# A decoder step in f32: fixed TensorE order in the prompt attention, gated products kept in PSUM, two tiles normed by VectorE

## The chip, the cores and the metric

One core of a Trainium2 chip runs one program. The metric is the time of one execution in device microseconds (us). The engines are PE (TensorE), DVE (VectorE), ACT (ScalarE), POOL (GpSimd) and SP (which issues most DMAs); PSUM has eight banks of 128 partitions, each of which takes 512 f32 columns here.

## The reference

One layer of a hybrid decoder serves a prompt of 1024 tokens and eight sample requests of eight tokens over paged caches. Cut to what matters here:

```
h  = x * (1 + scale1) + shift1
P  = h @ w_in                                  # conv part, queries, keys, values, gates
o  = gates * (compressed, selected and sliding-window attention)
x  = LN1(ALPHA * x + gate1 * (concat(rms(conv), rms(o)) @ w_o))
h2 = x * (1 + scale2) + shift2
x  = LN2(ALPHA * x + gate2 * (silu(h2 @ w_gate) * (h2 @ w_up)) @ w_down)
LN(x) = (x - mean(x)) * rsqrt(var(x) + EPS) * g + b
```

D_MODEL is 1024, the hidden width of the SwiGLU is 2816 (22 blocks of 128), there are 12 query heads of 64 over 2 key/value groups, and the sliding window is 512 keys. Everything is f32.

## The kernel before, in words

The stages follow one another: sample attention and compression to about 840 us, projections to 1041, the prompt attention (`phase_prompt`) to about 1441, `w_o` and the first norm to about 1565, and the feed-forward part with the second norm (`phase_ffn`) to the end.

**Prompt attention.** The work is cut into 32 units, a block i of 128 queries with one key/value group and one half of its heads; units go in 16 pairs. For each pair, `window()` interleaves two lists: the scores of the next pair and the values of this one. A chunk of scores is two matmuls into a bank of the pool `psS` (`khh`, then `kll`, lhsT are keys, `qs` the queries) and a DVE reduction (L1224) that adds the mask, takes the maximum and writes S to SBUF. ACT makes the exponentials (L1235), POOL combines the weights (L1247). `values()` then has, for each 128 keys, `tr(n)`: three PE transposes of S into a bank of `psPT` (L95) and one copy to an SBUF buffer `PT` of the pool `tp` (L1299, by ACT or DVE in turn); and `mm(n)`: two matmuls of PT with the values V, one into each half of the partitions of the one bank `psPO` (f32 rows, `V`, or `Vpc` for the compressed ones). `evac` and `out` take psPO out and turn it. The eight PSUM banks are psS 4, psPT 3, psPO 1. `both()` gives each value step a place LA steps behind its transposes, and a weight. These numbers (LA, FRONT, LEAD) set the order in which the code emits the work; a list scheduler then orders each engine's instructions by its own costs.

**Feed-forward.** The hidden blocks go in GROUPS: eight of two blocks and two of three. `down(n, i)` does one group for one tile i of 128 tokens: for each half of the 512 columns 6 (or 9) matmuls into one of five banks (psFD and psFG in turn), a DVE product with the gate (L1902) from PSUM to the SBUF row buffer `spare`, and a DVE `scalar_tensor_tensor` (L1903) that adds it into x. The last group goes by the order `g2 u2 g0 NT 6 u0 7 g1 0 1 u1 2 3 4 5`: gate and up blocks, and tiles by number (NT is the tile of the samples). After each tile's down, `finish(i)` takes the statistics (L1913, L1914) and `center()` (ACT square root, two small DVE operations L1650 and L1651, ACT identity L1652) makes x - mean times rstd in place; `write(i)`, one tile later, applies gain and bias (`affine`: POOL on the first columns at L1659 and DVE on the rest at L1661, 896 and 128 of 1024, but 768/256 for tile 4 and 256/768 for tile 5) and sends the tile out (L1921).

In the rows, `qo` names the rows of a tile of x (and `spare`), `fr` the gain and bias of the norm, `fst` the statistics, `fw`/`F` weights and hidden values, `gate1p` the gate.

Of the kernel before, what the change touches and what calls it, by code (L numbers as in the profile page):

```python
# [48 lines left out]
class _Step:  # L49
# [1121 lines left out]
    def phase_prompt(self):  # L1171
        nc, tc = self.nc, self.tc
        with ExitStack() as cx:
            pool = lambda n, b, **k: cx.enter_context(self.pool(n, b, **k))
            qp, tp = pool("pq", 6), pool("pt", 5)
            sp = [None, pool("pS1", 3)]
# [4 lines left out]
            extra = op.tile([P, D], F32, name="extra", tag="extra", bufs=1)  # L1181
            psS, psT, psO = (pool(n, b, space=PSUM) for n, b in (("psS", 4), ("psPT", 3), ("psPO", 1)))
            st = {}
# [154 lines left out]
            def both(a, b):  # L1338

                LA = 3  # L1340
                ta, ma, ea, oa = values(a)
                tb, mb, eb, ob = values(b)
                steps, at = [], {}
                for base, m in ((0, ma), (len(ta), mb)):
                    for k, f in enumerate(m):
                        at.setdefault(base + 2 * k + LA, []).append((0.7, f))
                end = 2 * len(ma) - 2 + LA
                at.setdefault(end, []).append((0.0, ea))
                at.setdefault(end + 3, []).append((0.4, oa))
                t = ta + tb  # L1350
                n = 0
                while n < len(t) or any(k >= n for k in at):
                    if n < len(t):
                        steps.append((0.33, t[n]))
                    steps += at.get(n, [])
                    n += 1
                return steps, [eb, ob]

            def window(sc, va, tail):

                tot = sum(x[0] or 0 for x in sc) + sum(x[0] for x in va)
                ev = [(0.1 + 1.4 * n, f) for n, f in enumerate(tail)]
                if sc:
# [18 lines left out]

            FRONT, LEAD = 0.6, 2.0
            for n in range(2):
# [5 lines left out]
            for n, pair in enumerate(pairs):  # L1390
# [4 lines left out]
                v, t = both(*pair)  # L1395
                window(nxt, v, tail)
                tail = t
# [248 lines left out]
    def center(self, x, m, st):  # L1646
# [3 lines left out]
        nc.vector.reciprocal(st[0:m, 15:16], st[0:m, 14:15])  # L1650
        nc.vector.scalar_tensor_tensor(st[0:m, 14:15], st[0:m, 12:13], -1.0, st[0:m, 15:16], op0=ALU.mult, op1=ALU.mult)  # L1651
        nc.scalar.activation(x[0:m, :], x[0:m, :], AF.Identity, bias=st[0:m, 14:15], scale=st[0:m, 15:16])  # L1652
# [146 lines left out]
    def phase_ffn(self):  # L1799
        nc, tc, I, O = self.nc, self.tc, self.I, self.O  # L1800
        gl = self.gl2
        with ExitStack() as cx:
# [84 lines left out]
            def down(n, i):  # L1887
# [3 lines left out]
                for h in range(2):  # L1891
                    c = slice(512 * h, 512 * h + 512)
                    ps = any_bank()
                    for j in range(a, b):
# [4 lines left out]
                        else:  # L1899
                            self.mm2(ps[:], f[:, T:TA + BS], w[:, 0, c], w[:, 1, c], j == a, j == b - 1)  # L1900
                    t = spare[:, c]
                    nc.vector.tensor_tensor(t, ps[:], g[:, c], op=ALU.mult)  # L1902
                    nc.vector.scalar_tensor_tensor(x[:, c], x[:, c], ALPHA if n == 0 else 1.0, t,  # L1903
                                                   op0=ALU.mult, op1=ALU.add)

            def finish(i):
# [7 lines left out]
                nc.vector.bn_aggr(st[0:m, 12:14], st[0:m, 0:12].rearrange("p (n c) -> p n c", n=2))  # L1914
                self.center(x, m, st)

            def write(i):
                m, x = P if i < NT else BS, self.x1[i]
                self.affine(x, m, *ln2, {5: (256, 256), 4: (768, 768)}.get(i, (896, 896)))
                dst = O[0][0, P * i:P * i + P, :] if i < NT else O[1].rearrange("b t d -> (b t) d")  # L1920
                nc.sync.dma_start(dst, x[0:m, :])  # L1921
# [48 lines left out]
            def last(i):  # L1970
                down(len(self.GROUPS) - 1, i)
                finish(i)
                if before:
                    write(before.pop())
                before.append(i)

            steps = ("g2", "u2", "g0", NT, 6, "u0", 7, "g1", 0, 1, "u1", 2, 3, 4, 5)
            for x in steps:
# [3 lines left out]
                else:  # L1982
                    last(x)
            write(before.pop())

# [70 lines left out]
```

## Time and profile before

| what | us |
|---|---|
| time, median of 3 runs | 2389.46 (2388.64 to 2394.4) |
| the profiled execution's own time | 2393.08 |
| its span | 2391.3 |
| PE busy | 2293.0, 96% of the span |
| DVE / ACT / POOL busy | 1429.6 / 920.1 / 851.7 |
| granted PE clock, mean | 0.99 |

Shares of busy time are averages over stages. The chain of work that ended last, followed back from the last instruction, lies on PE for 84% of the span and on DVE for 6%. In the 40 slices of the page PE is at nine tenths or more nearly everywhere; the last slice has four tenths. A start and a length of each instruction are printed by the timeline; PE's matmuls overlap, so the time that one takes from the path is the distance from its start to the start of the next, not its length.

### The profile page before, as it was taken

The page shows a single profiled execution, that of the slowest core. Times are in us where ns is not written, and L with a number is a line of the kernel's source. Part 1 is how long each engine was busy: PE and PEld are TensorE (multiplying, and loading weights), DVE is VectorE, ACT ScalarE, POOL GpSimd, SP SyncE. Part 2 cuts the span into 40 slices and gives each one's busy share as a digit, 9 for nine tenths or more (in the row PEclk, how much of TensorE's full clock was granted, in tenths as well). Part 3 has the DMA queues.
Part 4 walks back from the last instruction along what each step waited for, and adds up shares of the span by engine and source line. Part 5 has one row for each costly group of instructions (what it writes and reads, how often), then busy time and mean ns, then how long its engine had stood idle before and what let it go on. Part 6 is the DMA issues. An engine that isn't in the chain of part 4 may idle for free.

```text
span 2391.3 us, 38693 instructions
## 1 busy us (share of the span) xinstructions
PE 2293.0 (96%) x14834; PEld 1901.9 (80%) x14834; DVE 1429.6 (60%) x3407; ACT 920.1 (38%) x2108; POOL 851.7 (36%) x912
## 2 busy tenths in 40 slices
PE   5999999989999999999999999999999999999994
PEld 3777778778888788976566657889999999999893
DVE  4654766667777530167888776656554456552558
ACT  0232343348888512267767765331111111111122
POOL 6676766621111221244444453422212222212224
PEclk9999999999999999999999999999999999999997
DMA  9778555547665233100000013021111111111111
GB/s 285 263 269 281 201 169 175 172 160 267 249 249 220 84 132 82 47 28 1 1 1 1 1 45 102 28 61 45 45 36 53 45 45 45 45 36 54 41 37 68
DMA packets 139119, 249.23 MB, mean 104 GB/s; under 512 B 13507, under 2 KB 109741, under 8 KB 134774
## 3 DMA queue, kind: packets, MB, share of 16 engines
q0 software_dynamic: 23312, 138.36, 16.1%
q1 hardware_dynamic: 113446, 107.35, 14.5%
q8 instruction: 117, 1.92, 0.3%
q10 hardware_dynamic: 2176, 1.05, 0.2%
q14 instruction: 68, 0.56, 0.1%
HBM read 239.23 MB, written 11.63 MB: 105 GB/s over the span
## 4 chain that ended last, share of the span: by engine, by line
PE 84%; DVE 6%; DMA 2%; issue 2%; ACT 2%; POOL 2%; another core or an unknown queue 1%; SPq 0%; POOLq 0%; DVEq 0%; ACTq 0%
PE psFG L75 15%; PE psA L75 12%; PE psFU L75 11%; PE psM L75 7%; PE psPA L75 7%; PE psPO L75 6%; PE psS L75 5%; PE psFD L75 5%; PE psPT L95 5%; PE psST L95 4%; PE psWA L75 3%; PE psSO L75 2%; DVE qo L1661 1%; PE psM L95 1%
## 5 line engine op out<-in xcount | busy, mean ns | idle before, releaser
L72 POOL TENSOR_TENSOR fw<-fr,fw 128x1024 fp32r<-128x1024 f32 x64 | 160.9, 2520 | 584.8 <-ACT fw L66 584.8
L75 PE MATMUL psFU<-h,fw 128*128 128x384 f32 (+1 forms) x1056 | 252.5, 324 | 0.0
L75 PE MATMUL psFG<-h,fw 128*128 128x384 f32 (+1 forms) x1008 | 241.0, 324 | 0.0
L1247 POOL TENSOR_SCALAR S<-S,stat 128x64 f32<-128x64 f32 (+8 forms) x288 | 168.6, 602 | 191.4 <-DVE stat L1244 101.6
L623 DVE STREAM_TRANSPOSE XT<-X 128x1024 f32<-128x1024 f32 x128 | 158.9, 1242 | 124.5 <-PE psA L75 105.0
L66 ACT CAST fw<-fr 128x1024 fp32r<-128x1024 f32 x65 | 67.6, 1054 | 412.7 <-issue 305.4
L75 PEld LDWEIGHTS psFU<-h,fw 128*128 128x128 f32 x1056 | 190.6, 187 | 0.7
L625 POOL TENSOR_TENSOR XS<-XT 128x512 f32<-128x512 f32 x120 | 154.3, 1287 | 100.5 <-DVE XT L623 82.9
L1873 DVE TENSOR_TENSOR sl<-sl,psFU 128x384 f32<-128x384 f32 (+1 forms) x66 | 31.5, 527 | 259.9 <-PE psFU L75 257.6
L75 PEld LDWEIGHTS psFG<-h,fw 128*128 128x128 f32 x1008 | 182.2, 187 | 0.3 <-ACT sl L1861 0.2
L1235 ACT ACTIVATE S<-S,stat 128x64 f32<-128x64 f32 (+8 forms) x288 | 171.5, 598 | 18.7 <-DVE stat L1233 16.7
L1903 DVE SCALAR_TENSOR_TENSOR qo<-qo 128x512 f32<-128x512 f32 x180 | 174.9, 975 | 5.3
L75 PE MATMUL psFU<-h2a,fw 128*128 128x384 f32 x528 | 170.8, 338 | 0.0
L75 PE MATMUL psFG<-h2a,fw 128*128 128x384 f32 x504 | 166.4, 338 | 0.0
L75 PE MATMUL psA<-XT,wt 128*128 128x256 f32 x512 | 158.6, 392 | 3.4 <-DVE XT L623 3.4
L75 PE MATMUL psA<-XT,wb 128*128 128x256 f32 x512 | 154.5, 384 | 0.0
L75 PE MATMUL psA<-XS,ws 128*128 128x256 f32 x512 | 154.1, 383 | 0.0
L75 PE MATMUL psFD<-fw,F 128*128 128x512 f32 x572 | 145.9, 391 | 7.6 <-ACT F L1874 5.8
L75 PE MATMUL psFG<-fw,F 128*128 128x512 f32 x572 | 145.6, 392 | 0.0
L95 PE MATMUL psPT<-ident,S 128*128 128x128 f32 (+1 forms) x888 | 138.9, 277 | 1.4 <-POOL S L1247 0.9
L95 PEld LDWEIGHTS psPT<-ident,S 128*128 128x128 f32 (+1 forms) x888 | 101.8, 137 | 47.7 <-issue 28.6
L75 PE MATMUL psPO<-PT,V 128*64 128x384 f32 x528 | 133.4, 511 | 0.2
(488 smaller groups left out, 5318.4 us busy)
## 6 DMA issues: line engine op xcount, KB each, us to landing
wa<-in_w_ada_dram SPq DMA_DIRECT2D x48, 512.0 KB
fr<-in_w_ffn_up_dram SPq DMA_DIRECT2D x22, 512.0 KB
fr<-in_w_ffn_down_dram SPq DMA_DIRECT2D x22, 512.0 KB
fr<-in_w_ffn_gate_dram SPq DMA_DIRECT2D x21, 512.0 KB
wraw<-in_w_in_dram SPq DMA_DIRECT2D x32, 256.0 KB
qo<-in_x_prompt_dram SPq DMA_DIRECT2D x12, 512.0 KB
wa<-in_w_in_dram SPq DMA_DIRECT2D x10, 512.0 KB
Xw<-in_cache_win_kv_dram SPq DMA_DIRECT2D x8, 512.0 KB
```

The costliest lines, as they stand in the source:

```text
L66: self.last_act = nc.scalar.copy(hi, src)
L72: self.last_lo = e.tensor_tensor(lo, src, self.f32(hi), op=ALU.subtract)
L75: self.last_mm = self.nc.tensor.matmul(out, lhsT, rhs, start=start, stop=stop)
L95: self.nc.tensor.matmul(out, in_, self.ident[:n, :n], is_transpose=True, start=True, stop=True)
L623: nc.vector.transpose(out=x[:].rearrange("p u (t c) -> p (u t) c", t=4), in_=X[n][:, :, o:o + 128])
L625: (nc.gpsimd if n else nc.vector).tensor_tensor(t[:], x[:, 0], x[:, 1], op=ALU.add)
L1235: nc.scalar.activation(E[:, a:b], E[:, a:b], AF.Exp, bias=stat[:, s, 3 + br:4 + br], scale=SCALE, accum_out=stat[:, s, 6 + br:7 + br])
L1247: nc.gpsimd.tensor_scalar(E[:, a:b], E[:, a:b], stat[:, s, 9 + br:10 + br], 1.0, op0=ALU.mult, op1=ALU.mult)
L1661: nc.vector.tensor_tensor(x[0:m, :D - n], x[0:m, :D - n], v[0:m, :D - n], op=op)
L1873: nc.vector.tensor_tensor(sl[:, c], sl[:, c], pu[b][:, 0:n], op=ALU.mult)
L1903: nc.vector.scalar_tensor_tensor(x[:, c], x[:, c], ALPHA if n == 0 else 1.0, t, op0=ALU.mult, op1=ALU.add)
```

## The change

In the prompt attention: one bank moves from psS (4 to 3) to psPT (3 to 4), and `tp` has seven buffers instead of five. LA goes from 3 to 4, the value steps are emitted two at a time (`BURST`), `out` comes at end + 5 instead of end + 3, and the tail events of a pair stand 3.0 apart instead of 1.4. Around `window()` in the loop over pairs PE is under `manual_schedule`: its instructions go out in the order in which the code emits them, and the list scheduler orders only the other engines.

In the feed-forward part: the gated product is written back to its PSUM bank, and the add into x reads it there. Tiles 4 and 5 are normed within `finish`: (x - mean) * g in one DVE operation over 1024 columns, then per half (x * rstd + b) and a DMA of that half; they have no ACT identity and no `affine`. The `affine` of all other tiles is wholly POOL's. `center` makes one small product by `tensor_scalar` instead of `scalar_tensor_tensor`.

```diff
-            qp, tp = pool("pq", 6), pool("pt", 5)
+            qp, tp = pool("pq", 6), pool("pt", 7)
...
-            psS, psT, psO = (pool(n, b, space=PSUM) for n, b in (("psS", 4), ("psPT", 3), ("psPO", 1)))
+            psS, psT, psO = (pool(n, b, space=PSUM) for n, b in (("psS", 3), ("psPT", 4), ("psPO", 1)))
...
-                LA = 3
+                LA = 4
...
-                        at.setdefault(base + 2 * k + LA, []).append((0.7, f))
+                        if k % BURST == 0:
+                            fs = m[k:k + BURST]
+                            at.setdefault(base + 2 * (k + len(fs) - 1) + LA, []).append(
+                                (0.75 * len(fs), lambda fs=fs: [f() for f in fs]))
...
-                at.setdefault(end + 3, []).append((0.4, oa))
+                at.setdefault(end + 5, []).append((0.4, oa))
...
-                ev = [(0.1 + 1.4 * n, f) for n, f in enumerate(tail)]
+                ev = [(0.1 + 3.0 * n, f) for n, f in enumerate(tail)]
...
-            FRONT, LEAD = 0.6, 2.0
+            FRONT, LEAD, BURST = 0.6, 2.0, 2
...
-                window(nxt, v, tail)
+                with tc.manual_schedule(engines={mybir.EngineType.PE}):
+                    window(nxt, v, tail)
...
-                    t = spare[:, c]
-                    nc.vector.tensor_tensor(t, ps[:], g[:, c], op=ALU.mult)
-                    nc.vector.scalar_tensor_tensor(x[:, c], x[:, c], ALPHA if n == 0 else 1.0, t,
+                    nc.vector.tensor_tensor(ps[:], ps[:], g[:, c], op=ALU.mult)
+                    nc.vector.scalar_tensor_tensor(x[:, c], x[:, c], ALPHA if n == 0 else 1.0, ps[:],
                                                    op0=ALU.mult, op1=ALU.add)
...
-                self.center(x, m, st)
+                if i not in (4, 5):
+                    self.center(x, m, st)
+                    return
+
+                nc.scalar.activation(st[:, 14:15], st[:, 13:14], AF.Sqrt, bias=self.eps[:])
+                nc.vector.scalar_tensor_tensor(x[:], x[:], st[:, 12:13], ln2[0][:], op0=ALU.subtract, op1=ALU.mult)
+                nc.vector.reciprocal(st[:, 15:16], st[:, 14:15])
+                for h in range(2):
+                    c = slice(512 * h, 512 * h + 512)
+                    nc.vector.scalar_tensor_tensor(x[:, c], x[:, c], st[:, 15:16], ln2[1][:, c],
+                                                   op0=ALU.mult, op1=ALU.add)
+                    nc.sync.dma_start(O[0][0, P * i:P * i + P, c], x[:, c])
...
-                self.affine(x, m, *ln2, {5: (256, 256), 4: (768, 768)}.get(i, (896, 896)))
+                self.affine(x, m, *ln2, (D, D))
```

PE in the middle of the prompt attention, before (transposes into psPT, value matmuls into psPO with V or Vpc, score matmuls into psS):

```order
L75 MATMUL psPO<-PT,V_9691 64x384 x2
L95 MATMUL psPT<-ident,S 64x128 x3
L95 MATMUL psPT<-ident,S 128x128 x3
L75 MATMUL psPO<-PT,V_9692 64x384 x2
L75 MATMUL psS<-kll,qs 128x320
L95 MATMUL psPT<-ident,S 128x128 x3
L75 MATMUL psS<-khh,qs 128x480
L75 MATMUL psS<-kll,qs 128x480
L95 MATMUL psPT<-ident,S 128x128 x3
L75 MATMUL psS<-khh,qs 128x480
L75 MATMUL psS<-kll,qs 128x480
L75 MATMUL psPO<-PT,Vpc 64x384
```

The same stretch, after:

```order
L75 MATMUL psS<-khh,qs 128x320
L75 MATMUL psS<-kll,qs 128x320
L75 MATMUL psS<-khh,qs 128x256
L75 MATMUL psS<-kll,qs 128x256
L95 MATMUL psPT<-ident,S 128x128 x3
L75 MATMUL psPO<-PT,V_9691 64x384 x3
L75 MATMUL psPO<-PT,V_9692 64x384
L95 MATMUL psPT<-ident,S 128x128 x3
L95 MATMUL psPT<-ident,S 64x128 x3
L75 MATMUL psPO<-PT,V_9692 64x384 x4
L75 MATMUL psPO<-PT,Vpc 64x384
```

The value matmuls, two at a time and broken up by transposes before, now stand in runs of four, and two chunks of scores follow each other.

DVE near the end, tiles 2 and 3 of the last group, before (L1902/L1903 add a half of the down product into x, L1913/L1914/L1650/L1651 are the norm's statistics, L1661 is DVE's part of the affine):

```order
L1661 TENSOR_TENSOR qo<-qo,fr 128x128
L1903 SCALAR_TENSOR_TENSOR qo<-qo 128x512
L1661 TENSOR_TENSOR qo<-qo,fr 128x128
L1913 BN_STATS fst<-qo 128x6
L1902 TENSOR_TENSOR qo<-psFD,gate1p 128x512
L1914 BN_AGGR fst<-fst 128x2
L1903 SCALAR_TENSOR_TENSOR qo<-qo 128x512
L1650 RECIPROCAL fst<-fst 128x1
```

The last tiles, after (L1905/L1906 are the two operations of a half, L1916/L1917 the statistics, L1923 to L1927 the new norm of tiles 4 and 5):

```order
L1905 TENSOR_TENSOR psFD<-psFD,gate1p 128x512
L1916 BN_STATS fst<-qo 128x6
L1906 SCALAR_TENSOR_TENSOR qo<-qo,psFD 128x512
L1917 BN_AGGR fst<-fst 128x2
L1905 TENSOR_TENSOR psFG<-psFG,gate1p 128x512
L1923 SCALAR_TENSOR_TENSOR qo<-qo,fst,fr 128x1024
L1924 RECIPROCAL fst<-fst 128x1
L1906 SCALAR_TENSOR_TENSOR qo<-qo,psFG 128x512
L1927 SCALAR_TENSOR_TENSOR qo<-qo,fst,fr 128x512 x2
L1916 BN_STATS fst<-qo 128x6 x2
L1917 BN_AGGR fst<-fst 128x2
L1923 SCALAR_TENSOR_TENSOR qo<-qo,fst,fr 128x1024
```

DVE's part of the affine is gone from between the halves; the norm of tile 4 stands between the halves of tile 5.

## Rows read from the trace of the kernel before

**Rows 1.** Windows view: stretch, length, busy per engine (instructions), PE clock, DMA share, GB/s.

```profile
1064.00:1430.00 366.00, 365.04 (x2063) 220.83 (x2062) 292.22 (x1215) 256.56 (x734) 169.87 (x285) 1.00 0.02 7
1625.00:2295.00 670.00, 670.00 (x3665) 631.30 (x3664) 342.57 (x450) 99.93 (x167) 140.95 (x56) 1.00 0.15 45
2295.00:2344.00 49.00, 49.00 (x255) 44.31 (x253) 38.40 (x59) 14.23 (x20) 16.30 (x7) 1.00 0.11 38
```

**Rows 2.** PE timeline, prompt attention: start, length, engine, line, instruction, output<-input, shapes, count.

```profile
1201.03 0.87 PE L75 MATMUL psPO<-PT,V 128*64 128x384 f32 x4
1201.83 0.41 PE L75 MATMUL psS<-kll,qs 128*128 128x320 f32 x1
...
1202.63 0.38 PE L75 MATMUL psS<-kll,qs 128*128 128x480 f32 x1
1202.84 0.49 PE L95 MATMUL psPT<-ident,S 128*128 128x128 f32 x3
...
1203.39 0.38 PE L75 MATMUL psS<-kll,qs 128*128 128x480 f32 x1
1203.70 0.85 PE L75 MATMUL psPO<-PT,Vpc 64*64 64x384 f32 x2
1204.49 0.42 PE L75 MATMUL psS<-khh,qs 128*128 128x320 f32 x1
1204.74 0.31 PE L75 MATMUL psS<-kll,qs 128*128 128x320 f32 x1
1204.89 0.49 PE L95 MATMUL psPT<-ident,S 128*128 128x128 f32 x3
```

**Rows 3.** DVE timeline, the same stretch: the reductions of two chunks.

```profile
1203.74 0.59 DVE L1224 CUSTOM_DVE_ANT_0 S<-psS,mz 128x416 f32<-128x416 f32 x1
...
1204.83 0.72 DVE L1224 CUSTOM_DVE_ANT_0 S<-psS,mz,stat 128x480 f32<-128x480 f32 x1
```

**Rows 4.** DVE and POOL timelines, a down step in mid feed-forward.

```profile
1701.00 2.77 DVE L1903 SCALAR_TENSOR_TENSOR qo<-qo 128x512 f32<-128x512 f32 x1
1703.69 0.68 DVE L1902 TENSOR_TENSOR qo<-psFG,gate1p 128x512 f32<-128x512 f32 x1
...
1705.01 0.68 DVE L1902 TENSOR_TENSOR qo<-psFD,gate1p 128x512 f32<-128x512 f32 x1
...
1700.83 2.40 POOL L72 TENSOR_TENSOR fw<-fr,fw 128x1024 fp32r<-128x1024 f32 x1 [10.35 <-ACT fw L66]
```

**Rows 5.** Line views of L1902 and L1903: count, min/median/max ns, first and last start.

```profile
L1902 DVE TENSOR_TENSOR qo<-psFD,gate1p x80: 632/684/692, 1628.7 to 2373.2; 128x512 f32<-128x512 f32 x80
...
L1903 DVE SCALAR_TENSOR_TENSOR qo<-qo x180: 672/693/2889, 1629.4 to 2375.9; 128x512 f32<-128x512 f32 x180
```

**Rows 6.** PE timeline, the end: in brackets the idle time before, and its releaser.

```profile
2338.39 2.24 PE L75 MATMUL psFD<-fw,F 128*128 128x512 f32 x9
...
2349.87 1.22 PE L75 MATMUL psFD<-fw,F 128*128 128x512 f32 x2 [5.85 <-ACT F L1874]
2352.85 0.80 PE L75 MATMUL psFD<-fw,F 128*128 128x512 f32 x1 [1.75 <-DVE F L1878]
2353.44 3.51 PE L75 MATMUL psFG<-fw,F 128*128 128x512 f32 x9
...
2362.91 2.20 PE L75 MATMUL psFG<-fw,F 128*128 128x512 f32 x9
```

**Rows 7.** DVE, POOL and SP-queue timelines, the end.

```profile
2311.99 1.22 DVE L1911 TENSOR_TENSOR qo<-qo 64x1024 f32<-64x1024 f32 x1 [1.11 <-ACT qo L1910]
...
2346.03 2.04 DVE L1661 TENSOR_TENSOR qo<-qo,fr 128x128 f32<-128x128 f32 x1
...
2357.37 0.69 DVE L1913 BATCH_NORM_STATS2 fst<-qo 128x6 f32<-128x512 f32 x1
...
2368.08 2.56 DVE L1903 SCALAR_TENSOR_TENSOR qo<-qo 128x512 f32<-128x512 f32 x1
...
2361.53 4.41 POOL L1659 TENSOR_TENSOR qo<-qo,fr 128x896 f32<-128x896 f32 x2 [6.79 <-ACT qo L1652]
...
2385.27 0.33 SPq L1921 DMA_DIRECT2D out_dram<-qo  x1
```

More of the change, by code (lines that the diff above doesn't have):

```diff
@@ L1650, in center @@
         nc.vector.reciprocal(st[0:m, 15:16], st[0:m, 14:15])
-        nc.vector.scalar_tensor_tensor(st[0:m, 14:15], st[0:m, 12:13], -1.0, st[0:m, 15:16], op0=ALU.mult, op1=ALU.mult)
+        nc.vector.tensor_scalar(st[0:m, 14:15], st[0:m, 12:13], st[0:m, 15:16], -1.0, op0=ALU.mult, op1=ALU.mult)
         nc.scalar.activation(x[0:m, :], x[0:m, :], AF.Identity, bias=st[0:m, 14:15], scale=st[0:m, 15:16])
@@ L1974, in last @@
                     write(before.pop())
-                before.append(i)
+                if i not in (4, 5):
+                    before.append(i)
             steps = ("g2", "u2", "g0", NT, 6, "u0", 7, "g1", 0, 1, "u1", 2, 3, 4, 5)
@@ L1983, in phase_ffn @@
                     last(x)
-            write(before.pop())
     def merge(self, a, b):
```

## The prediction

> **What bounds the kernel now.** I read the 40 slices first (PE is nearly always full), then the windows of the three stages that the change touches, then timelines. In the prompt attention from 1064 to 1430 us PE is busy for 365.04 of 366 us at a granted clock of 1.00, beside DVE with 292.22 (80%) [rows 1]. So this stage is as long as PE's own work, and only what makes PE's work shorter, or makes PE wait, moves it; but DVE has just a fifth of its time free. In mid feed-forward PE is busy for 670.00 of 670 us and DVE for 342.57 [rows 1]: a change on DVE there gives nothing and costs nothing while DVE keeps up. At the end it is otherwise: PE waits 5.85 and 1.75 us for F, which ACT and DVE had late [rows 6], and DVE is late because operations that read two SBUF operands take 2.04 us for 128 columns (L1661) or 2.56 us for 512 (L1903) beside POOL's affine, against 0.69 for the same L1903 alone [rows 5, 7]. From PE's last matmul (2362.91 + 2.20 = 2365.1) to the last DMA's issue at 2385.27 [rows 6, 7] the end belongs to DVE, ACT and POOL; 6.0 us follow from that issue to the span's end at 2391.3.
>
> **Prompt attention: what PE saves.** PE's matmuls overlap, so prices are distances between starts [rows 2]. A pair of value matmul steps (psPO, x4) takes 1201.03 to 1201.83 = 0.80 us; a single step (x2) takes 1203.70 to 1204.49 = 0.79, the same. So two steps next to each other cost what one alone costs, as they fill the two halves of the partitions at once. Counted over the stage in the program order of PE, pairs and single steps are 117 + 62 = 179 before and 134 + 28 = 162 after: 17 fewer, at 0.75 (the lower side of 0.80) some 13 us. Second, going in and out of a group of value matmuls costs something: `kll` of 480 columns takes 1202.63 to 1202.84 = 0.21 ahead of transposes and 1203.39 to 1203.70 = 0.31 ahead of a value group, +0.10; a 320-column score matmul takes 1204.49 to 1204.74 = 0.25 behind a group and 1204.74 to 1204.89 = 0.15 otherwise, +0.10. That is 0.20 us for each group. The order has 173 unbroken groups before and 81 after: 92 × 0.20 = 18.4, say 19 with the bounds 14 and 23 (0.15 and 0.25 a group). Together PE's work in the stage falls by about **32 us**, some 8%.
>
> **Prompt attention: what may be given back.** A fixed order means that PE waits wherever the next instruction's bank or operand is late; the scheduler had left no more than 1 us of that in 366 [rows 1]. The bank moved away from psS decides. A score bank is free when DVE's reduction of that chunk is over. From the `kll` at 1202.63 to the end of its reduction (1203.74 + 0.59 = 1204.33) it is 1.70 us, from the one at 1203.39 to 1204.83 + 0.72 = 1205.55 it is 2.16 [rows 2, 3]. Priced along the order with the distances above, a bank's next use comes a median of 3.9 us after its last matmul before, and 2.6 us after the change; nearer than 1.7 us it comes in 2 of 269 cases before, and in 58 after. If each of these 58 waits 0.2 us (half way from 0 to the 0.4 or so by which the slower reduction of the two passes 1.7) that is 12 us, less what one wait spares the next; I take **10**. What lies on the other side: the bank added to psPT and LA = 4 make copies less urgent. Value matmuls that come within 1.6 us of their transposes fall from 42 to 16 of 296, so no new wait is taken for them, and seven PT buffers cover the longer distance. `out` two steps later and the tails 3.0 apart move DVE and PE work by a few us within a stage that has no end of its own there: nothing. Sum of the stage: −32 + 10 = **−22**. Bounds: −32 (no waits) to 0 (R1), and beyond in R3.
>
> **Mid feed-forward.** A half's two DVE operations take 1703.69 to 1705.01 = 1.32 us [rows 4], while PE needs 1.36 for its six matmuls (2.04 × 6 / 9, by 2.04 from start to start of nine near the end). The bank is now held until L1903's successor has read it. There are five banks, psFD's two in every other half, so that the half before last of a step of 18 halves waits for the DVE work of 13: PE waits only if 1.46 + 13 D > 16 × 1.36, that is if a half takes DVE over D = 1.56 us. With 1.32 there is no wait: **0**. L1902 already reads PSUM and SBUF: 684 ns median and never over 692, beside the L1903 with two SBUF operands, 693 and up to 2889 [rows 5]; the 2.77 us one runs just while POOL's L72 runs [rows 4]. So the new add, which is of L1902's kind of operands, should lose those long cases. Writing a product to PSUM is in no row here; the bounds are −0.1 and +0.4 us an operation, at the upper end D = 1.9 and 4.4 us of waiting in each of eight groups, 35 us; I take the near end, as L1902's reading side shows no surcharge.
>
> [...]
>
> **The end.** PE starts tile 2 at 2338.39 [rows 6]. The 5.85 and 1.75 us of waits and 3.51 − 2.20 = 1.31 of the nine slow matmuls behind them [rows 6] go away when DVE is free of L1661 and of the long L1903: PE ends about 8.9 us earlier, near 2356. What is late next is DVE itself. It begins on tile 2 at about 2340.6. Per half it has 1.32 + 0.69 for the statistics [rows 4, 7], per tile 4.0 + 0.5 of small operations: four tiles are 18.0. Tiles 4 and 5 have each one operation of 1024 columns (1.22, by L1911, which is the nearest row [rows 7]), a reciprocal of 0.12, and two halves of 0.7: 2.75 each, of which 5.5 in all. 2340.6 + 18.0 + 5.5 = 2364.1, about 2365 with the square root on ACT between. The issue at 2385.27 thus moves to about 2365 and the span's end, 6.0 later, to 2371: **−20**. POOL's affine of tile 3 over 1024 columns takes 4.41 × 1024 / 896 = 5.0 us [rows 7]; it starts near 2352 and is over before tile 5's norm. But the new L1923 and L1927 read two SBUF operands each: in the worst case three of them wait 2 us (rows as L1661's 2.04) and a DMA behind them too, −14; with 6.0 shortened by half-sized DMAs, −22. `center`'s small product (0.15 us) is nothing.
>
> **The sum.** 2393.08 − 22 − 20 = 2351.1 for an execution like the profiled one. This lies 3.6 above the median of the runs, so on the scale of the medians I say **2347** (2389.46 − 42 = 2347.5), with a band of 2337 (−32 and −22, or 2335) to 2358.
>
> **The rivals.**
> R1: three score banks give the prompt gain back. For it speaks that DVE's 80% become 292 / 334 = 87% if the stage is 32 us shorter, and 58 near reuses instead of 2; against it that the median distance of 2.6 us is still above both lags. It needs 32 us of waits, 0.12 us at each of some 270 reuses. Time: 2389.5 − 20 = 2369.
> R2: the end gives half. The two-SBUF waits move to L1923 and L1927, or the PSUM operand does not spare L1903's successor the long cases. Time: 2347 + 10 = 2357.
> R3, slower: the third score bank's waits go beyond the gain. Each wait also delays the transposes behind it in the fixed order, hence the copies, hence the values, and nothing can step ahead. It decides from a mean wait of about 0.2 us on each of 270 reuses (52 us, what stage and end give together); at 0.3 it is 81 us: 2389.5 − 32 − 20 + 81 = 2418. Against it: only a fifth of the reuses are near.
> R4: transposes and the clock. Before, the granted clock was 1.00 over a stage full of transposes [rows 1]; the longest unbroken run of them in the order goes from 11 to 21. If PE fell to its lower level in such a run, the price is that of the nine matmuls after the waits, 1.31 us [rows 6]; once in each of 16 pairs, 21 us: 2368. [...]
> R5: it does not do what it says (the group price of 0.20 was something else, and the end is set by another queue): 2389.
>
> **How the numbers follow.** Forecast (2335 to 2358) 0.66; R1 0.14; R2 0.08, inside or at the edge of the band; R3 0.06; R4 0.03; R5 0.03. The range 2333 to 2370 holds the forecast, R2, R4 and about half of what scatters about R1, and leaves out R3, R5 and the upper side of R1, 0.06 + 0.03 + 0.07 = 0.16. About 0.3% (7 us) is what a measurement of this kernel can tell from no change: faster by more are the forecast, R1, R2 and R4, 0.91; within 0.3% R5, 0.03; slower R3, 0.06.
>
> **What would show it.** Right: the stage from 1041 on about 22 us shorter, with PE's matmul starts as dense as before but for some 10 us of idle time that psS or DVE's L1224 releases; value groups in half the number; mid feed-forward equal to 1 us, the L1906 never much over 0.7 us; the last issue 20 us nearer to the start of tile 2's down. Wrong: idle time before score matmuls of 30 us and more (R1, R3); a clock under 1.00 between 1064 and 1410 (R4); idle time of PE before psFD in mid feed-forward; L1923 or L1927 of over 2 us (R2).

## The result, and the profile after

The changed kernel takes 2345.64 us in the median of 4 runs (2344.55 to 2349.68), the kernel before 2389.05 (2388.21 to 2394.4, 4 runs): a ratio of 0.9818, with a 95% interval of 0.9805 to 0.9832. Predicted were 2347.

The two profiled executions differ by 2391.3 - 2343.2 = 48.1 us of span. Four marks in the timelines of PE cut both spans into stages: the first score matmul (psS), the first matmul of the feed-forward part (psFG), the first down matmul of tile 2 (psFD, behind the last up block), and the end.

| stage | before | after | difference | predicted |
|---|---|---|---|---|
| ahead of the first score matmul | 1040.9 | 1033.7 | -7.2 | 0 |
| prompt attention, to the first w_o matmul (psWA) | 399.4 | 379.2 | -20.2 | -22 |
| w_o and first norm, to psFG | 113.2 | 116.2 | +3.0 | 0 |
| feed-forward, to tile 2's last down | 784.9 | 784.6 | -0.3 | 0 |
| the end | 52.9 | 29.4 | -23.4 | -20 |

The first row is not put down to the change: in fourteen traces of this study that stage lies anywhere between 1033.5 and 1044.2, with the code there the same, and two traces of the changed kernel itself have 1033.7 and 1040.2. It is most of the difference between executions, so a stage of the trace tells smaller differences than a median of totals does. How small differs: the end repeats to 0.1 us in five traces with the same code there. In what follows, "prompt with w_o" is the sum of the second and third row: 512.6 before; in two runs with only a feed-forward part changed 512.3 and 511.0; after, in five traces with the same changed prompt part (two of the changed kernel, three with one thing undone or varied in its feed-forward part), 495.4 to 498.0, mean 496.6; the prompt part alone has 497.3.

The prompt attention in three stretches (first 24 us, middle, last 20 to 23 us), windows view, columns as in [rows 1], first after:

```profile
1033.60:1058.00 24.40, 18.53 (x78) 14.34 (x79) 21.24 (x111) 17.60 (x62) 16.18 (x36) 0.79 0.13 42
1058.00:1390.00 332.00, 328.61 (x2015) 219.90 (x2013) 282.60 (x1207) 252.62 (x727) 162.85 (x275) 1.00 0.01 3
1390.00:1413.00 23.00, 17.82 (x120) 10.65 (x118) 14.34 (x28) 9.20 (x20) 6.63 (x8) 0.93 0.27 89
```

and before:

```profile
1040.80:1065.00 24.20, 22.09 (x99) 14.81 (x100) 22.37 (x122) 18.91 (x66) 16.50 (x37) 0.93 0.12 43
1065.00:1420.00 355.00, 354.42 (x2001) 214.93 (x1999) 284.64 (x1196) 253.08 (x726) 163.65 (x277) 1.00 0.01 3
1420.00:1440.30 20.30, 19.17 (x113) 9.55 (x112) 14.12 (x25) 7.78 (x18) 6.88 (x8) 1.00 0.51 168
```

In the middle PE now waits 3.4 us of 332, against 0.6 of 355 before: the fixed order is nearly as dense as the scheduler's. At the two ends it waits 5.9 and 5.2 us, against 2.1 and 1.1, and the mean granted clock is lower there, 0.79 and 0.93 against 0.93 and 1.00. From the first score matmul to the first w_o matmul, before and then after:

```profile
1040.91:1440.32 399.41, 395.70 (x2208) 239.31 (x2209) 321.12 (x1342) 279.67 (x808) 186.93 (x319) 1.00 0.04 13
1033.71:1412.90 379.19, 364.86 (x2208) 244.78 (x2208) 318.06 (x1344) 279.31 (x807) 185.55 (x317) 0.98 0.03 11
```

With the same 2208 instructions PE is busy for 364.86 us instead of 395.70, 30.8 less, and idle for 14.3 instead of 3.7, 10.6 more. What PE waits for in the stage after the change, waits view (sum, times, longest):

```profile
PE psWA L75 <- DVE mT L72: 4.1, 1, 4.1
PE psS L75 <- DVE stat L1224: 3.5, 6, 1.9
PE psPT L95 <- DVE stat L1242: 2.8, 1, 2.8
PE psS L75 <- DVE stat L1233: 0.8, 3, 0.3
```

The longest are a single one at the start (the first pair's weights, 2.8) and a single one at the end (the first w_o matmul waits for mT, 4.1); score banks (psS), by L1224 and L1233, cost 4.3 in nine waits, against 1.0 in three before. The value groups, answering to [rows 2], PE timeline:

```profile
1376.71 1.59 PE L75 MATMUL psPO<-PT,V 128*64 128x384 f32 x8
1378.22 0.43 PE L75 MATMUL psS<-khh,qs 128*128 128x352 f32 x1
...
1386.78 2.51 PE L75 MATMUL psPO<-PT,V 128*64 128x384 f32 x12
```

Two pairs in one group take 1378.22 - 1376.71 = 1.51 us, against 0.80 for one.

Mid feed-forward, windows and line views, answering to [rows 1, 5]:

```profile
1589.00:2270.00 681.00, 681.00 (x3731) 642.33 (x3731) 301.74 (x457) 102.12 (x171) 136.65 (x57) 1.00 0.15 45
```

```profile
L1905 DVE TENSOR_TENSOR psFD<-psFD,gate1p x80: 682/700/700, 1604.0 to 2328.3; 128x512 f32<-128x512 f32 x80
...
L1906 DVE SCALAR_TENSOR_TENSOR qo<-qo,psFD x90: 672/686/690, 1604.8 to 2329.5; 128x512 f32<-128x512 f32 x90
L1906 DVE SCALAR_TENSOR_TENSOR qo<-qo,psFG x90: 661/686/690, 1606.2 to 2332.2; 128x512 f32<-128x512 f32 x90
```

The add took up to 2889 ns before and 690 at most now, over the same 180 instructions. The end, PE, DVE and SP-queue timelines, answering to [rows 6, 7]:

```profile
2313.75 2.24 PE L75 MATMUL psFD<-fw,F 128*128 128x512 f32 x9
...
2328.07 2.20 PE L75 MATMUL psFG<-fw,F 128*128 128x512 f32 x9
...
2330.92 1.28 DVE L1923 SCALAR_TENSOR_TENSOR qo<-qo,fst,fr 128x1024 f32<-128x1024 f32 x1
...
2332.77 2.83 DVE L1927 SCALAR_TENSOR_TENSOR qo<-qo,fst,fr 128x512 f32<-128x512 f32 x2
...
2338.47 1.42 DVE L1927 SCALAR_TENSOR_TENSOR qo<-qo,fst,fr 128x512 f32<-128x512 f32 x2
...
2334.97 5.28 SPq L1929 DMA_DIRECT2D out_dram<-qo  x4
```

PE runs its eight halves without a wait (no bracket between 2313.75 and 2328.07 + 2.20), then DVE works on until 2339.89, and the span ends 3.3 us later.

### The profile page after: what moved, and what is told of

Its sections match the earlier page's. It is cut to its first block, busy times and chain, and to the rows that moved or that the text cites. A ratio compares the mean times of both kernels' runs of the same rounds, so it can differ in the third digit from the quotient of the medians.

```text
span 2343.2 us, 38665 instructions
## 1 busy us (share of the span) xinstructions
PE 2258.1 (96%) x14834; PEld 1907.0 (81%) x14834; DVE 1360.0 (58%) x3393; ACT 918.7 (39%) x2108; POOL 841.6 (36%) x908
## 3 DMA queue, kind: packets, MB, share of 16 engines
q0 software_dynamic: 23312, 138.36, 16.5%
## 4 chain that ended last, share of the span: by engine, by line
PE 86%; DVE 6%; POOL 2%; issue 2%; DMA 2%; ACT 2%; DVEq 0%; SPq 0%; POOLq 0%; ACTq 0%
PE psFG L75 17%; PE psA L75 12%; PE psFU L75 11%; PE psM L75 8%; PE psPA L75 7%; PE psFD L75 6%; PE psST L95 5%; PE psPO L75 5%; PE psS L75 4%; PE psPT L95 4%; PE psWA L75 3%; PE psSO L75 3%; DVE S L1224 1%; PE psM L95 1%; DMA wa<-in_w_ada_dram 1%
## 5 line engine op out<-in xcount | busy, mean ns | idle before, releaser
L72 POOL TENSOR_TENSOR fw<-fr,fw 128x1024 fp32r<-128x1024 f32 x64 | 154.1, 2415 | 591.3 <-ACT fw L66 591.3
L95 PE MATMUL psPT<-ident,S 128*128 128x128 f32 (+1 forms) x888 | 132.7, 276 | 3.8 <-DVE stat L1242 2.8
L288 POOL DMA_INDIRECT X<-in_cache_cmp_kv_dram,idxc x120 | 120.1, 1001 | 28.4 <-issue 19.4
L75 PE MATMUL psS<-khh,qs 128*128 128x320 f32 (+10 forms) x312 | 121.2, 392 | 6.1 <-DVE stat L1224 3.5
L75 PE MATMUL psPA<-hTh,wsp 128*128 128x512 f32 x384 | 125.3, 400 | 1.8 <-DVE hTh L68 1.7
```

The lines of the kernel that those rows point to most:

```text
L72: self.last_lo = e.tensor_tensor(lo, src, self.f32(hi), op=ALU.subtract)
L75: self.last_mm = self.nc.tensor.matmul(out, lhsT, rhs, start=start, stop=stop)
L95: self.nc.tensor.matmul(out, in_, self.ident[:n, :n], is_transpose=True, start=True, stop=True)
L288: nc.gpsimd.indirect_dma_start(out=X[n][:, k], out_offset=None, in_=cache, in_offset=bass.IndirectOffsetOnAxis(ap=self.idxc[:, k // 4, c:c ...
```

## The experiments

Twelve runs followed, one of them the changed kernel again. This table has each median and, from its trace, the two stages that the change moved; the ratios are in the text.

| kernel | median us | prompt with w_o | end |
|---|---|---|---|
| before | 2389.05 | 512.6 | 52.9 |
| after | 2345.6 | 495.4 | 29.4 |
| prompt part only | 2373.8 | 497.3 | 52.9 |
| norm and affine only | 2376.2 | 512.3 | 40.9 |
| PSUM product only | 2384.4 | 511.0 | 48.3 |
| after, free order | 2373.3 | 520.1 | 29.4 |
| after, bank back | 2350.9 | 493.8 | 29.4 |
| after, BURST 1 | 2372.9 | 518.5 | 29.4 |
| after, product in SBUF | 2356.2 | 498.0 | 36.9 |
| after, `center` as before | 2350.8 | 496.7 | 33.5 |
| after, one DMA a tile | 2350.3 | 496.2 | 29.7 |
| after (again) | 2352.7 | 496.7 | 29.4 |
| norm in PSUM, longer lead | 2346.7 | 495.1 | 28.2 |
| the same, bank back | 2344.4 | 491.9 | 28.2 |

**One part alone, three times.** The prompt part (all of the diff in `phase_prompt`):

```diff
...
-                window(nxt, v, tail)
+                with tc.manual_schedule(engines={mybir.EngineType.PE}):
+                    window(nxt, v, tail)
```

> Only the prompt attention's part of the change is made: fixed order of PE, bursts, the bank moved; the feed-forward part is as before. Theory (PE's own work falls, by 92 value groups fewer at 0.20 us and 17 value slots fewer at 0.75, and some 10 us come back as waits): 2389 - 17 to 22, 2367 to 2372. In the two traces the stretch from the first score matmul to the first matmul of the feed-forward part was 17.2 us shorter after the change, so 2372 is the likeliest. Rival (7.2 us that the traces differ by ahead of the prompt attention belong to the change as well, by where its code lies): 2365. Rival (the two parts need each other): 2380 or more.

Measured: 0.9934 (0.9915 to 0.9953), 2373.8, and 497.3 us for prompt with w_o. The first theory holds to within 2 us (2372 was the likeliest); the rival that gave it the 7.2 us ahead falls, since its first score matmul comes at 1039.7.

The norm of tiles 4 and 5 and the affine on POOL:

```diff
...
-                self.affine(x, m, *ln2, {5: (256, 256), 4: (768, 768)}.get(i, (896, 896)))
+                self.affine(x, m, *ln2, (D, D))
...
```

> Only the norm of tiles 4 and 5 on DVE and the affine wholly on POOL; the product stays in SBUF (spare). Theory (the end is longer by DVE's two-SBUF operations beside POOL and by a serial norm of tile 5): L1661's long cases (some 7 us) and the chain from the last statistics at 2376.6 to the last issue at 2385.3 are gone, L1903's long cases (some 4 us in sum) stay: 2389 - 23.5 + 6 = 2372. Rival (the parts need each other, since POOL's affine of 5 us a tile now lies beside nearly all adds, 8 halves with 2 us more): 2382.

Measured: 0.9953 (0.9939 to 0.9966), 2376.2, an end of 40.9 us: between the two. Four of the last eight adds are long, as the theory said, 1.46 to 2.17 us and 4.1 more in sum than at 0.69 each. Two things come on top that it did not name: the first operation of tile 4's new norm takes 3.35 us instead of 1.28, and L1651 is held up too. Its DVE and PE timelines:

```profile
2338.08 2.08 DVE L1651 SCALAR_TENSOR_TENSOR fst<-fst 128x1 f32<-128x1 f32 x1
...
2341.89 0.73 PE L75 MATMUL psFD<-fw,F 128*128 128x512 f32 x2 [1.46 <-ACT F L1874]
```

L1651 is the product of one column in `center`, 0.15 us when alone. Here it takes 2.08 while POOL does an affine (and 1.57 for a later tile), the up block's DVE operation queues behind it, and PE waits 1.46 us for F.

The product in PSUM:

```diff
...
-                    nc.vector.tensor_tensor(t, ps[:], g[:, c], op=ALU.mult)
+                    nc.vector.tensor_tensor(ps[:], ps[:], g[:, c], op=ALU.mult)
...
```

> Only the gated product in its PSUM bank. Theory (an operation with one PSUM operand isn't held up by POOL): every add takes 0.7 us, none over 0.8; mid feed-forward equal; at the end the long L1903 (1.86, 1.87, 2.56 us) are gone and L1661's stay: 2389 - 4 = 2385. Rival (PSUM operations cost more in a row of 18 halves, D over 1.56 us, so that PE waits for a bank in mid feed-forward): 2395 or more. Rival (POOL holds up the next two-SBUF operation instead, so nothing is won): 2389.

Measured: 0.9981 (0.9969 to 0.9993), 2384.4; mid feed-forward equal to 1 us, the end 4.6 us shorter. The theory holds.

The two ends do not add up: -12.0 and -4.6 make -16.5 where the whole makes -23.4, and 6.9 us are missing. `center`'s line is in neither of them, and the two parts need each other; two runs below take the line and the product out of the whole, at 4.1 us for the one and 7.5 for the other, 2.9 more than the product gave alone.

**What makes the prompt attention shorter.** First, the changed kernel without the fixed order:

```diff
-                with tc.manual_schedule(engines={mybir.EngineType.PE}):
-                    window(nxt, v, tail)
+                window(nxt, v, tail)
```

> The changed kernel, but the list scheduler orders PE in the prompt attention (no fixed order; banks, bursts, LA as changed). In its program order there are 130 value groups (81 with the fixed order) and 195 value slots (162). Theory (PE's own work by the prices 0.20 a group and 0.75 a slot): + 10 + 25 = 35 us less the 10 or so of waits that a free order avoids: 2346 + 25 = 2371. Rival (the order isn't what counts but the bank for transposes and the longer distances): 2346 to 2350. Rival (the free order avoids waits and loses little): under 2346.

Measured: 2373.3, 0.9932 (0.9913 to 0.995); prompt with w_o 520.1, that is 23.5 more than the mean of after and 7.5 more than before the change. Then the fixed order with steps one at a time:

```diff
-            FRONT, LEAD, BURST = 0.6, 2.0, 2
+            FRONT, LEAD, BURST = 0.6, 2.0, 1
```

> The changed kernel with value steps emitted one at a time (BURST 1), the order still fixed. 148 value groups instead of 81 and 168 slots instead of 162. Theory (0.20 us a group, 0.75 a slot): 13.4 + 4.5 = 18 us more in the prompt attention, 2364. Rival (the groups cost nothing, only the fixed order and the banks count): 2346 to 2350, by the slots alone.

Measured: 2372.9, 0.9921 (0.9906 to 0.9936); prompt with w_o 518.5, 21.9 more than after, where 18 was expected. Of what the median is over 2364 beyond that, much lies ahead of the stage: in the trace its first score matmul comes at 1041.4, 7.7 us after that of the changed kernel. So the fixed order alone and the bursts alone each lose all of the gain: only the order that keeps the bursts together has it. Both runs come out as was expected from the count of groups and slots, at 0.20 and 0.75 us, to within 4 us. In the free order two errors cancel in part: up to the first w_o matmul PE is busy for 394.8 us, 29.9 more than after the change where the count has 35, and its waits are 5.6 us less, not 10. LA, the seven buffers of `tp` and the later `out` and tail events were not taken out alone. What causes the 0.10 us on each side of a group [rows 2], no run shows.

**The bank that was moved.**

```diff
-            psS, psT, psO = (pool(n, b, space=PSUM) for n, b in (("psS", 3), ("psPT", 4), ("psPO", 1)))
+            psS, psT, psO = (pool(n, b, space=PSUM) for n, b in (("psS", 4), ("psPT", 3), ("psPO", 1)))
```

> The changed kernel with four score banks and three for transposes, as before the change. PE's own work by the program order is about 2 us less (77 groups, 160 slots). Theory A (a third score bank costs what the trace shows, 4.3 us of waits for L1224 and L1233, and bursts of up to 21 transposes need the fourth transpose bank): the waits before score matmuls go to near 0, waits before transposes for their copies come, 5 to 10 us: 2350 to 2355. Theory B (the bank for transposes isn't needed): 2340 to 2343.

Measured: 2350.9, 0.9836 (0.9821 to 0.9851). The median is theory A's, the stage theory B's: 493.8, less than in any of the five with the bank moved. The waits move as A says:

```profile
PE psPT L95 <- ACT PT L1299: 5.7, 11, 1.0
...
PE psPT L95 <- DVE PT L1299: 2.0, 4, 1.1
PE psS L75 <- DVE stat L1224: 1.2, 2, 0.9
```

7.7 us for transposes that wait for a copy instead of 0.5, and 1.2 instead of 3.5 for score banks. But the order is another one (77 groups, 160 slots), and the first w_o matmul no longer waits. That holds throughout: in the nine traces with the bank moved, of the free order too, this matmul waits 2.0 to 5.8 us for mT, and in the five with four score banks not at all. So the wait at this seam goes with the bank, or with the order of emission that it brings, and not with the fixed order. The last pair of runs below repeats the comparison: 491.9 against 495.1. In both comparisons the moved bank is some 3 us worse, by one trace each with the bank back, where the same code spreads over 2.6 us; the times cannot tell it (2350.9 against 2345.6 and 2352.7; 2344.4 against 2346.7).

**What makes the end shorter.** The product back in SBUF, all else as changed:

```diff
-                    nc.vector.tensor_tensor(ps[:], ps[:], g[:, c], op=ALU.mult)
+                    t = spare[:, c]
+                    nc.vector.tensor_tensor(t, ps[:], g[:, c], op=ALU.mult)
...
```

> The changed kernel with the gated product back in the SBUF row buffer. Mid feed-forward as before (PE waits for nothing). Theory (an add with two SBUF operands is held up while POOL's affine runs, which is nearly always from tile 2 on): as in the run with the norm alone, four or so of the last eight adds take 1.5 to 2.2 us instead of 0.7, and L1923 up to 3.3 instead of 1.3; the end is 5 to 7 us later: 2351. Rival (the PSUM product is neutral): 2346.

Measured: 0.9853 (0.9838 to 0.9868), 2356.2; the end is 36.9, 7.5 longer. The median is 5 us over the theory's; in the trace the first score matmul comes 5.4 us later than in that of the changed kernel. DVE's timeline (L1907 is the add, L1924 the first operation of the new norm):

```profile
2326.59 2.17 DVE L1907 SCALAR_TENSOR_TENSOR qo<-qo 128x512 f32<-128x512 f32 x1
...
2330.11 1.46 DVE L1907 SCALAR_TENSOR_TENSOR qo<-qo 128x512 f32<-128x512 f32 x1
...
2344.94 3.35 DVE L1924 SCALAR_TENSOR_TENSOR qo<-qo,fst,fr 128x1024 f32<-128x1024 f32 x1
```

Six of the last eight adds take 1.3 to 2.2 us where 0.69 is the time alone, and the norm's first operation takes 3.35 instead of 1.28. Then the one line of `center`:

```diff
-        nc.vector.tensor_scalar(st[0:m, 14:15], st[0:m, 12:13], st[0:m, 15:16], -1.0, op0=ALU.mult, op1=ALU.mult)
+        nc.vector.scalar_tensor_tensor(st[0:m, 14:15], st[0:m, 12:13], -1.0, st[0:m, 15:16], op0=ALU.mult, op1=ALU.mult)
```

> The changed kernel with one line undone: the product of mean and rstd of 128 x 1 in center is again a scalar_tensor_tensor instead of a tensor_scalar. The prediction held this edit for nothing (0.15 us against 0.2). Theory, new since the run with the norm alone, where this line took up to 2.08 us with a median of 0.74 (0.15 alone): a scalar_tensor_tensor is held up beside POOL even at one column, and DVE, which paces the end, is 3 to 5 us later: 2349 to 2351. Rival (it is nothing): 2346.

Measured: 0.984 (0.9819 to 0.9861), 2350.8, and an end of 33.5 us, 4.1 longer. The line's view, in this kernel and then in the changed one:

```profile
L1655 DVE SCALAR_TENSOR_TENSOR fst<-fst x7: 143/1324/2236, 2299.6 to 2334.1; 128x1 f32<-128x1 f32 x6, 64x1 f32<-64x1 f32 x1
```

```profile
L1655 DVE TENSOR_SCALAR fst<-fst x7: 197/208/216, 2293.6 to 2326.4; 128x1 f32<-128x1 f32 x6, 64x1 f32<-64x1 f32 x1
```

Seven instructions of one column: a median of 1.32 us in one form, 0.21 in the other. Three of the seven had POOL idle beside them and took 0.14 or 0.15 us; the four beside the affine took 1.32 to 2.24, and each of them ended within 0.03 us of the end of the POOL instruction that was running. The longest, with the two POOL instructions up to then (timelines of POOL and DVE):

```profile
2331.47 4.89 POOL L1663 TENSOR_TENSOR qo<-qo,fr 128x1024 f32<-128x1024 f32 x2 [2.83 <-ACT qo L1656]
2334.14 2.24 DVE L1655 SCALAR_TENSOR_TENSOR fst<-fst 128x1 f32<-128x1 f32 x1
```

The POOL row ends at 2331.47 + 4.89 = 2336.36, the DVE row at 2336.38. So what these four lost is what was left of POOL's instruction (2.40 us in the median of the 14 of the changed kernel), though the operation of DVE itself takes 0.15 us. Of the 4.1 us this row is 2.1; of the rest, L1923 of tile 4 now meets the affine and takes 3.43 instead of 1.28, while L1927 behind it takes 0.73 instead of 2.17.

In the timelines of the end, the DVE operations that took long beside POOL all read two tensor operands from SBUF; among them are the add with its product in SBUF (up to 2.56 us before the change, 0.69 alone), the first operation of the new norm (up to 3.43, 1.28 alone), and `scalar_tensor_tensor` on two columns of the statistics (up to 2.24, 0.15 alone). The add with its product in PSUM, which reads one from SBUF, took 0.69 at most in the 180 cases of the changed kernel, and the small product as `tensor_scalar` 0.22 at most.

**What follows the last operation.**

```diff
-                    nc.sync.dma_start(O[0][0, P * i:P * i + P, c], x[:, c])
+                nc.sync.dma_start(O[0][0, P * i:P * i + P, :], x[:])
```

> The changed kernel, but tiles 4 and 5 are each sent out by one DMA after both halves instead of one for each half. Theory (the last transfer's size sets what follows the last operation: 6.0 us before with a whole tile, 3.3 us after with half a tile): the last operation ends as before, the span 2.7 us later: from the start of tile 2's down to the end 32.1 us instead of 29.4. Rival (the 3.3 us comes from something else, as the queue being empty): 29.4 to 30.

Measured: an end of 29.7 instead of 29.4, 0.2 us (the median, 2350.3, can't tell it). The theory falls: the size of the last transfer is worth 0.2 us, not 2.7. Windows of the last microseconds, before and then after (last column GB/s):

```profile
2386.00:2388.00 2.00, 0.00 (x0) 0.00 (x0) 0.00 (x0) 0.00 (x0) 0.00 (x0) 0.50 0.66 262
2388.00:2390.00 2.00, 0.00 (x0) 0.00 (x0) 0.00 (x0) 0.00 (x0) 0.00 (x0) 0.50 0.00 0
2390.00:2391.30 1.30, 0.00 (x0) 0.00 (x0) 0.00 (x0) 0.00 (x0) 0.00 (x0) 0.50 0.00 0
```

```profile
2340.00:2342.00 2.00, 0.00 (x0) 0.00 (x0) 0.00 (x0) 0.00 (x0) 0.00 (x0) 0.50 0.71 262
2342.00:2343.20 1.20, 0.00 (x0) 0.00 (x0) 0.00 (x0) 0.00 (x0) 0.00 (x0) 0.50 0.00 0
```

A whole tile's bytes take the same time, 2.27 us from the issue to the last of them before and 2.26 in this run; before, the span goes on for over 3 us after them, with no engine busy and no transfer at work. Over the fourteen traces, from the last DMA's issue to the end: 6.01 us in the three in which POOL's affine ends within 0.1 us of that issue (before, prompt part only, PSUM product only), 3.30 to 3.32 or, with a whole tile, 3.53 in the eleven in which POOL was done at least 5 us earlier. The traces show what makes the difference: the DRAIN in POOL's queue, the first instruction of its closing line, which the busy columns leave out. POOL's last affine and the view of that line (count, min/median/max ns, first and last start), before and then after:

```profile
2382.36 2.89 POOL L1659 TENSOR_TENSOR qo<-qo,fr 128x256 f32<-128x256 f32 x2 [1.90 <-ACT qo L1652]
L2052 POOLq DRAIN  x3: 46/97/6596, 2383.9 to 2391.0; - x3
```

```profile
2323.75 10.64 POOL L1663 TENSOR_TENSOR qo<-qo,fr 128x1024 f32<-128x1024 f32 x4 [0.99 <-ACT qo L1656]
L2066 POOLq DRAIN  x3: 46/97/8614, 2331.0 to 2342.9; - x3
```

The long one is the first of the three. Before, it ends at 2383.9 + 6.6 = 2390.5, 5.24 us after POOL's last affine; after, at 2339.6, again 5.24. These 5.24 us are the same in all fourteen traces, and the span ends some 0.8 us after the later of two things: this DRAIN, or SP's last wait, which is over 2.5 us after the issue of half a tile and 2.8 after that of a whole one. Before, the DRAIN is later; with POOL's work 5.5 us ahead of the last issue the transfer is.

**Further.** The changed kernel again, as a measure for the two beside it:

> The changed kernel once more, as the measure for the two runs beside it: 2346, the stretch from the first score matmul to the feed-forward part 495 to 498 us, and the end from tile 2's down 29.4 us.

It gave 2352.7 (0.9847, 0.9826 to 0.9869) in that set of runs, 7 us over the first set, with the stages as expected (496.7 and 29.4); 6.5 us of the two profiled executions' difference lie ahead of the first score matmul (1040.2 against 1033.7).

Then x of tiles 4 and 5 kept in PSUM through their norm, and more score work ahead of the first values:

```diff
-                    nc.vector.scalar_tensor_tensor(x[:, c], x[:, c], ALPHA if n == 0 else 1.0, ps[:],
+                    nc.vector.scalar_tensor_tensor(ps[:] if held else x[:, c], x[:, c], ALPHA if n == 0 else 1.0, ps[:],
...
-                    window(nxt, v, tail)
+                    window(nxt, v, tail, LEAD if n else 6.0)
```

> The changed kernel carried further: x of tiles 4 and 5 stays in its PSUM banks from the last add on, so that no operation of their norm reads two SBUF operands; and 6.0 instead of 2.0 of score work stands ahead of the first pair's values. Theory (what holds DVE up at the end is two SBUF operands beside POOL): L1927's pair, 2.83 us for tile 4 after the change, takes 1.4; the end is 1 to 1.4 us shorter, 28.2 instead of 29.4; the wait of 2.8 us for the first weights goes, the prompt stretch is 2 to 3 us shorter. Together 2342. Rival (PSUM operands cost as much as the hold-up, and the first pair waits elsewhere): 2346.

Measured: 2346.7, 0.9829 (0.9809 to 0.9848), 6 us under the changed kernel beside it. The end is 28.2, as the theory says; DVE's timeline of tile 4:

```profile
2332.30 0.74 DVE L1935 SCALAR_TENSOR_TENSOR qo<-psFD,fst,fr 128x512 f32<-128x512 f32 x1
2332.96 0.74 DVE L1935 SCALAR_TENSOR_TENSOR qo<-psFG,fst,fr 128x512 f32<-128x512 f32 x1
```

1.4 us for the pair that took 2.83. The longer lead gave next to nothing: the wait of 2.8 us for the first weights is gone, but score banks cost 4.8 instead of 3.5, the first w_o matmul waits 5.8 instead of 4.1, and the stage is 495.1, 0.3 under the lowest of the five. Last, the same with the bank back:

> As the run with the norm in PSUM and the longer lead, with four score banks and three for transposes. In the trace with the bank back the stretch from the first score matmul to the feed-forward part was 493.8 us, against 495.4 to 498.0 in four traces with the bank moved (one of them, with the prompt part alone, 497.4), while the median was 5 us higher. Theory (the bank is neutral or a little better where it was): 2 us shorter stretch than the run beside it, 2340 to 2342. Rival (the median was right, the moved bank is worth 5 us): 2347.

Measured: 2344.4, 0.9821 (0.9799 to 0.9843), the lowest median of the study in a set in which the changed kernel had 2352.7. The stage is 491.9, 3 us less than beside it.

## Why the prediction was right, step by step

**PE's work in the prompt attention, -32.** Right: PE is busy for 30.8 us less up to the first w_o matmul. Taken out of the whole, the bursts cost 21.9 us (18 by the count) and the fixed order 23.5 (25 by the count and the waits).

**What is given back, +10.** The size was right (10.6), the place wrong, and so the size was luck. The term was 58 near reuses of score banks at 0.2 us; score banks cost 4.3 us, 3.3 more than before. The rest came at two places that had no term: the first pair's weights (2.8) and the seam to w_o, where PE waits 4.1 us for mT, then 1.0 and 1.3 more (0.6 twice before), at a granted clock of 0.93 in the last 23 us and 0.98 in the stage behind, 1.00 in both before. The attention itself, from the first score matmul to its last transposes, became 25.2 us shorter (399.4 to 374.2); 8.0 of these are lost again between there and the feed-forward part (113.2 to 121.3). That leaves 17.2 less, where 22 less was predicted.

**Mid feed-forward, 0.** Right: PE is busy for 681.00 of 681 us. A half takes 0.700 + 0.686 us, under the 1.56 from which, by the prediction's estimate, PE would wait for a bank. (The upper bound there is summed wrongly: 0.4 on each of two operations makes 2.12, not 1.9, and 58 us of waiting, not 35; and the -0.1 and +0.4 us an operation were the author's guess, which no row shows. The forecast did not use them.) Measured are 16 ns more for the product that now also writes to PSUM, and 7 ns less for the add (700 against 684 and 686 against 693 in the median).

**The end, -20.** It was -23.4. DVE's path was right to 0.5 us: from the start of tile 2's down to the last operation 2364.1 or 2365 - 2338.39 = 25.7 to 26.6 predicted, 2339.89 - 2313.75 = 26.1 measured. Mis-sized was the term behind it, 6.0 us, taken from the row of before: it measured 3.3. The 6.0 were not the DMA's but POOL's DRAIN, and the change itself moved POOL's last work 5.5 us ahead of the last issue; the half-sized DMAs, which the prediction named for this, are worth 0.2. And one edit was held for nothing that is worth 4.1 us, `center`'s small product. The sum hid it: the prediction reckoned with DVE work that is never held up beside POOL but at L1923 and L1927, which is true only with that edit. The line view of before had it, in its maximum:

```profile
L1651 DVE SCALAR_TENSOR_TENSOR fst<-fst x9: 134/148/1405, 2317.6 to 2380.8; 128x1 f32<-128x1 f32 x8, 64x1 f32<-64x1 f32 x1
```

That is 0.15 us in the median of nine, and 1.4 at most.

**The rivals.** R1 and R3 (score banks) fall: 4.3 us of waits, not 32 or 81. R2 falls for the whole, but its mechanism is real, and its sign came: the two-SBUF waits did move to L1927, whose first half of tile 4 takes 2.17 us (2.83 for the pair). R4 falls: that a long run of transposes lowers the clock was the author's supposition, and no trace shows it. The granted clock is 1.00 from 1058 to 1390 us, with the longest runs of transposes in it; it was 0.79 and 0.93 in the stretches ahead of that and behind, where PE waited 5.9 and 5.2 us. R5 falls.

**The median.** It came 43.4 lower, where -42 was predicted; the changed stages sum to 41 in the traces, so part of the closeness is that the parts' errors (-3.4 at the end, +4.8 at the prompt with w_o) cancel. Part is luck of the set of runs too: in the last set the same kernel was 35.5 us under the kernel before beside it (2352.7 against 2388.1), with the two stages of its trace the same to 1.3 us.

## What to carry to other kernels

When one engine is dense, price its instructions by the distance between starts for each kind of neighbour, and count neighbours in the program order: that priced two new orders to within 4 us of some 500. Here a fixed order saved only together with the grouping that it protects. Of the 10.6 us of idle time that the new order and banks added, 7.9 stand in the first and last 25 us of the stage, so read these and the start of the next. Beside a busy POOL, look at the maximum and not at the median of every DVE operation with two SBUF operands, down to one column (here 2.24 us against 0.15 alone), and move one operand to PSUM (here an add of 0.69 us at most, where it had taken up to 2.89) or into a scalar slot, an operand of one value per partition, as `tensor_scalar` takes it (here 0.22 at most). And end POOL's work early: here its DRAIN would be the later one at the end if POOL's last instruction ended less than 2.4 to 2.7 us ahead of the last DMA's issue, an estimate from the 5.24 and the 2.5 to 2.8 us above.

## What the runs showed of the hardware

- A `scalar_tensor_tensor` of 128 x 1 with both columns in SBUF took up to 2.24 us beside POOL's affine and 0.14 or 0.15 with POOL idle; the same product as `tensor_scalar` never over 0.22. Each of the four that were held up ended within 0.03 us of the POOL instruction beside it.
- A single step of value matmuls into half the partitions cost 0.79 us, a pair into both halves 0.80, and two pairs in one group 1.51.
- POOL's closing DRAIN ended 5.24 us after POOL's last operation in all fourteen traces. From the last DMA's issue to the end of the span it was 6.01 us where POOL worked to the end, and 3.31 where it had finished at least 5 us earlier; a whole tile instead of two halves cost 0.2.
- The same code took up to 10.7 us more or less, between traces, ahead of the first score matmul, and by 2.6 us at most in the stage that was compared.
